# One TensorE step per retention chunk: outputs, update and scores joined, orders planned anew

## The chip, the cores and the metric

The kernel runs on one core of a Trainium2 chip. The metric is device time of one execution in microseconds (us). The engines are TensorE (PE in the profile; its weight loads PEld), VectorE (DVE), ScalarE (ACT), GpSimd (POOL) and the queue of SyncE (SP), which issues nearly all DMA transfers. Each engine works through its own instructions in the order of the program and waits on semaphores for the others.

## The reference

One layer with two head groups side by side. The input is normalised, one projection gives all columns, the groups are gated and mapped back:

```python
h = rms_norm(x, norm_w)
rq, rk, rv, rg, sq, sk, sv, sg = split(h @ w_in)
# A) retention, 4 heads, dk 64, dv 128, 16 chunks of 128 tokens
scores = einsum('bhnid,bhnjd->bhnij', qc, kc) * decay
intra  = einsum('bhnij,bhnje->bhnie', scores, vc)
kv     = einsum('bhnjd,bhnje->nbhde', kc * zeta, vc)
prev   = scan(state = chunk_decay * state + kv_n)     # the state before each chunk
cross  = einsum('bhnid,nbhde->bhnie', qc * xi, prev)
ro = group_norm(intra + cross) * ret_norm_w * silu(rg)
# B) attention in a sliding window of 128, 8 heads over 2 key heads, bias, sinks
so = sliding_window_attention(sq, sk, sv, ...) * silu(sg)
x = x + concat(ro, so) @ w_out
```

There are 2048 tokens and 1024 model columns, all in float32.

## The kernel before

*The big products.* The four projections (three column ranges of w_in, then w_out) are made by Strassen's seven products of half-size blocks, over 8 pairs of token chunks. Each factor is split into a high and a low part (fp32r), and three products of parts make one. They appear in the profile as `acc<-w,x`: 128-row, 128-column products with 512, 384 or 256 columns of result. The splits (`x<-x`, `w<-w`) and the additions around them are work of ScalarE and VectorE.

*Between them* lies the rest, in small products on parts of the array: for each chunk a turn of the keys (`m<-ident,kn`), the attention logits (`m<-ks,qT`, 64x32 parts, in two halves of 32 records in the trace), for each pair of chunks the attention values (`m<-pT,vn`, 32x64 parts), and for each chunk of the retention, on 64x64 parts, in halves of 64 tokens:

- *update*: keys times values (`m<-v,qk`), for each half of the chunk; VectorE adds each to the running state (`state`), two additions of 128x256 for a chunk; for every fourth chunk ScalarE rescales the state (`base`);
- *scores*: keys times queries within each half (`m<-qkT`), and the queries times the state before each half (`m<-state,qkT`); VectorE then multiplies the scores by a triangle (`sT<-m,tri`), two instructions;
- *outputs*: the scores times the values (`m<-v,sT`), accumulated onto the cross products in the same two banks of PSUM; ScalarE moves them out (`ro<-m`, one instruction for one bank and two for the other), VectorE takes their statistics, and once in four chunks follows the group norm.

Queries and keys reach TensorE turned (`qkT`): ScalarE sorts their 16-bit halves apart (`apart`), a transfer stores them (`planes_dram<-apart`), and a transposing transfer brings them back. The values of a chunk are two loads (`v0`, `v1`).

*What sets the order.* The whole program is a list of operations, each with an estimated cost on its engine, its buffers and a due time; `Program.emit` (lines 176 to 329) plays a schedule and writes the instructions of all five engines in the order that it finds, once and for all. It holds back an operation whose buffers are not free; buffers come from shared counts (`SHARE`, `CAP`), PSUM has eight banks, of which small products may hold six (`"rest": 6`) and the big ones three. Operations of TensorE that use parts of the array carry a mark (`"quarters"`, `"eighths"`, `"bands"`); a change between marks, or to none, is charged `CHANGE` or `LESSER`, and `LATER`, `CROWD`, `MOST` and `SOONER` decide how long such an operation may be put off to stand beside another one. `AHEAD` and `SPARE` set how early a load may be issued. `HELD` names results that stay in SBUF instead of going through DRAM, `TURNED` what is turned by DMA. `WIN`, `RET`, `GATE` and `LEAD` (lines 1541 to 1545) are the due times of attention, retention and gates.

In `retention` (from line 907) one loop over the 16 chunks issues, for each, loads, the rotary phase, the key scales and the turn, and then update, state additions, scores, decays, outputs and evacuation, each as an operation of its own. So each chunk has three operations of TensorE, `update` (line 1004), `scores` (line 1051) and `outputs` (line 1075), due at different times and put where the schedule finds room. All instructions pass through one helper, so the profile gives line 421 for nearly every one; the names of the tiles tell them apart.

Of the kernel before, what the change touches and what calls it, by code (L numbers as in the profile page):

```python
# [33 lines left out]
AF = mybir.ActivationFunctionType  # L34
# [28 lines left out]
SHARE = {"x": 8, "raw": 64, "acc": 59, "wr": 32, "wh": 18, "att": 47, "ret": 41, "rin": 56, "gate": 13, "mix": 28, "norm": 5, "res": 3, "turned": 6, "vn": 3, "first": 5, "block": 3, "rest": 6}  # L63
# [3 lines left out]
AHEAD, SPARE, SPARED = 14.0, 3, ("raw", "wr")  # L67
# [36 lines left out]
LATER, CROWD, MOST, SOONER = 0.25, 0.25, 5, 142.0  # L104
# [239 lines left out]
HELD = {"sums": ((3, 1), (5, 4), (5, 5), (6, 3), (6, 6), (7, 0), (7, 1), (7, 5)), "ro": (1, 4, 6, 9, 12, 13, 14, 15), "q": (0, 2, 3, 13, 14), "gates": (4, 7), "so": (2, 5, 15)}  # L344
# [25 lines left out]
def small(n=1):  # L370
    return {"V": (0.2 * n, 0.28 * n, True)}
# [22 lines left out]
VALUES = {"T": (2.05, 2.27, False)}  # L394
# [30 lines left out]
def layer(ctx, tc, xt, xfirst, xtok, nw, w_in, w_rn, qkw, sinks, biasg, rope, decays, dmask, gpow, w_out, out):  # L425
# [33 lines left out]
    def ps(share="rest", name="m"):  # L459
        return Buf("bank", None, F32, name, share)  # L460
# [446 lines left out]
    def retention(at):  # L907
# [15 lines left out]
        state = None  # L923
        st = None
        for c in range(NCH):
# [61 lines left out]
            halves = (slice(0, 64), slice(64, 128))  # L987

            last = c == NCH - 1
            pkv = [ps() for _ in range(1 if last else 2)]  # L990

            def go(e, pkv=pkv, qk=qk, v=v):
# [9 lines left out]
            news = [hb("state") for _ in pkv]  # L1002
# [4 lines left out]
            states = [state]  # L1007
            for p, new in zip(pkv, news):
                old = states[-1]
                op(  # L1010
                    {"V": dve(256)},
                    lambda e, new=new, p=p, old=old: e.tensor_tensor(new(), p()[:, 0:256], old(), ALU.add)
                    if old else e.tensor_copy(new(), p()[:, 0:256]),
                    [p] + [old] * (old is not None), [new], due - 0.5, label="state",
                )
                states.append(new)
            state = states[-1]
            if c % BASED == BASED - 1 and not last:

                def go(e, state=state):  # L1020
                    for pr in range(2):
                        s = state()[:, pr * P : (pr + 1) * P]
                        e.activation(s, s, AF.Copy, scale=gp()[:, pr : pr + 1])

                op({"A": (0.45, 0.55, False)}, go, [state, gp], [state], due - 0.4, label="base")

            pros, sT = [ps(), ps()], hb("sT")
            sTs = [Part(sT, lambda t, i=i: t[:, i * P : (i + 1) * P]) for i in range(2)]

            def go(e, pros=pros, qkT=qkT, states=states):  # L1030
# [22 lines left out]
            for i in range(2):  # L1053
                op(
                    {"V": dve(128)},
                    lambda e, sT=sTs[i], pro=pros[i]: e.tensor_tensor(
                        sT().rearrange("p (a k) -> p a k", a=2), pro()[:, 256:384].rearrange("p (a k) -> p a k", a=2),
                        tri().unsqueeze(1).to_broadcast([P, 2, HALF]), ALU.mult,
                    ),
                    [pros[i], tri], [sTs[i]], due + 0.5, label="decay", also=(sT,),  # L1060
                )

            def go(e, pros=pros, sTs=sTs, v=v, c=c):
# [14 lines left out]
            ro = kb("ro", "mix" if c in HELD["ro"] else "ret")  # L1078
            for i, moves in enumerate([[(slice(0, P), slice(0, P))], [halves, halves[::-1]]]):

                def go(e, ro=ro, pro=pros[i], i=i, moves=moves):
                    for to, of in moves:
                        e.activation(
                            ro()[to, :].rearrange("p (a b d) -> p a b d", a=2, b=2)[:, :, i, :],
                            pro()[of, 0:256].rearrange("p (a d) -> p a d", a=2), AF.Copy,
                        )

                n = len(moves)
                op({"A": (0.307 * n, 0.31 * n + 0.11, False)}, go, [pros[i]], [ro], due + 0.7, label="ro")
            if c % NORMED == 0:  # L1090
                st, ros = sb("st", [P, NORMED, RH, 6]), []
            ros.append((c, ro))

            def go(e, st=st, ro=ro, c=c):
                for h in range(RH):
                    e.bn_stats(st()[:, c % NORMED, h, :], ro()[:, h * P : (h + 1) * P])

            op({"V": (0.8, 0.9, False)}, go, [ro], [st], due + 0.8, label="stats")
            if c % NORMED == NORMED - 1:
                group_norm(st, ros, due + 1)  # L1100
# [81 lines left out]
    def values(c, held, due):  # L1182
# [29 lines left out]
        for k in range(2):  # L1212
# [9 lines left out]
            op({"A": (0.95, 1.05, False)}, go, pavs, [so], due + 2.1, label="so")  # L1222
# [55 lines left out]
    def attend(c, a, b, fac, facs, due, bias_t, ks_t, nsnk):  # L1278
# [112 lines left out]
        for g in range(KVH):  # L1391
            if slot == 0:
                wholes[g] = wide("pT")
            lg, pT = lgs[g], Part(wholes[g], lambda t: t[:, slot * 640 : slot * 640 + 640])
            op(
                {"V": (0.85, 0.95, False)}, lambda e, lg=lg, pT=pT: e.transpose(pT(), lg()), [weights_of[g], weights_of[2 + g]], [pT],
                due + 1.3 + 0.3 * g, label="turn weights", also=(lg, wholes[g]),
            )
            pTs.append(pT)
# [128 lines left out]
    retention(lambda c: RET[0] + c // 2 * 2 * RET[1] + c % 2 * 1.0)  # L1528
# [12 lines left out]
WIN = (58.0, 4.8)  # L1541
RET = (126.5, 2.15)
GATE = (139.0, 5.45)

LEAD = 12.0
# [95 lines left out]
```

## Time and profile before

| | us |
|---|---|
| three timed runs | 675.07, 679.26, 678.53 |
| their median | 678.53 |
| the profiled execution | 676.0 |
| its span in the trace | 674.2 |
| TensorE busy, of the span | 667.9 |
| VectorE busy | 592.8 |
| ScalarE busy | 475.0 |

The profile is of one execution. A row of a view by groups gives the operation, the tiles that it writes and reads, the shape, the count, the busy time and the mean duration of one in ns, and the idle time ahead with what ended it. A row of the timeline gives start, duration, engine and the merged instructions. Each small fp32 product of the program shows as two records of TensorE, so a group of eight products has 16. Durations in the timeline overlap, since the products are pipelined; differences of starts do not.

### The profile page before, as it was taken

Reading aid. Unit: us, or ns where it says so; the run is one execution under the profiler, and the core shown is the slowest. Engines: PE = TensorE matmul, PEld = TensorE weight load, DVE = VectorE, ACT = ScalarE, POOL = GpSimd, SP = SyncE. Lnnn points to the kernel's source line nnn. Section 1 sums busy time; section 2 is a strip of 40 time slices with the busy share of each in tenths; the row PEclk is TensorE's granted clock in tenths of the full one; section 3 lists DMA queues with packets and bytes.
Section 4 is the critical chain, followed back from the end, with each engine's and each line's share of the span. In section 5 each row is a group of like instructions: output and inputs, shape, how many; then the busy total and the mean of one; then the engine's idle time right before and its main releaser. Section 6 shows DMA issues by size and latency. Waiting matters only on the chain.

```text
span 674.2 us, 16326 instructions
## 1 busy us (share of the span) xinstructions
PE 667.9 (99%) x5948; PEld 558.8 (83%) x5948; DVE 592.8 (88%) x1369; ACT 475.0 (70%) x1145; POOL 17.7 (3%) x39
## 2 busy tenths in 40 slices
PE   9999999999999999999999999999999999999998
PEld 7887888888989999998887777777788888888886
DVE  6998967887899988899999989998899999987782
ACT  7663798657797776787989799897999944533300
POOL 0000000033200000000000000000000000000000
PEclk9999999999999999999999999999999999999999
DMA  9976598978975899999989879988996886015652
GB/s 328 367 230 221 180 360 276 344 242 298 251 214 160 253 269 287 310 282 318 270 213 285 234 243 281 197 276 231 313 256 209 224 205 195 17 64 192 215 186 94
DMA packets 154145, 161.65 MB, mean 240 GB/s; under 512 B 67793, under 2 KB 95313, under 8 KB 154065
## 3 DMA queue, kind: packets, MB, share of 16 engines
q1 hardware_dynamic: 153920, 160.60, 79.3%
q8 instruction: 47, 0.77, 0.5%
q14 instruction: 34, 0.27, 0.1%
q10 hardware_dynamic: 144, 0.00, 0.0%
HBM read 97.05 MB, written 49.35 MB: 217 GB/s over the span
## 4 chain that ended last, share of the span: by engine, by line
PE 89%; DMA 4%; DVE 3%; ACT 1%; issue 1%; SPq 0%; DVEq 0%; ACTq 0%
PE acc L421 78%; PE m L421 12%; DMA aq_dram<-r 1%; DMA s_dram<-x 1%; DMA aq_dram<-t 1%; DVE w L421 1%; DVE x L421 1%; DMA xk<-in_xtok 1%; DVE t L421 0%; SPq L421 0%; DMA x<-in_xt 0%; ACT sq L421 0%; DVE s L421 0%; DVE hs L421 0%; ACT x L421 0%
## 5 line engine op out<-in xcount | busy, mean ns | idle before, releaser
L421 PE MATMUL acc<-w,x 128*128 128x512 f32 (+1 forms) x2700 | 594.8, 378 | 0.8 <-ACT x L421 0.4
L421 PEld LDWEIGHTS acc<-w,x 128*128 128x128 f32 x2700 | 490.5, 188 | 89.6 <-issue 7.4
L421 DVE TENSOR_TENSOR x<-x 128x512 fp32r<-128x512 f32 (+2 forms) x220 | 143.5, 674 | 10.6 <-ACT x L421 7.4
L421 ACT ACTIVATE x<-x 128x512 fp32r<-128x512 f32 (+1 forms) x187 | 111.7, 616 | 23.3 <-DVE x L421 15.1
L421 ACT ACTIVATE lg<-lg,nm 128x160 f32<-128x160 f32 x128 | 53.1, 418 | 12.2 <-DVE nm L421 12.2
L421 DVE TENSOR_TENSOR w<-w 128x512 fp32r<-128x512 f32 (+3 forms) x96 | 60.9, 655 | 0.0
L421 DVE SCALAR_TENSOR_TENSOR w<-w,nw_sb 128x512 fp32r<-128x512 f32 (+3 forms) x72 | 49.4, 702 | 1.0 <-ACT w L421 1.0
L421 DVE TENSOR_TENSOR s<-acc,s 128x512 f32<-128x512 f32 (+1 forms) x64 | 41.7, 652 | 8.4 <-PE acc L421 7.7
L421 ACT ACTIVATE w<-w 128x512 fp32r<-128x512 f32 (+1 forms) x72 | 40.7, 599 | 10.3 <-PE acc L421 6.5
L421 DVE CUSTOM_DVE_ANT_0 lg<-m,bias,nsnk 128x160 f32<-128x160 f32 x128 | 40.6, 379 | 5.5 <-PE m L421 5.2
L421 DVE TENSOR_TENSOR r<-acc,t 128x512 f32<-128x512 f32 (+1 forms) x32 | 20.9, 654 | 15.3 <-PE acc L421 13.9
L421 DVE TENSOR_TENSOR t<-acc,t 128x512 f32<-128x512 f32 (+2 forms) x33 | 21.1, 638 | 13.2 <-PE acc L421 12.9
L421 ACT ACTIVATE s<-acc 128x512 f32<-128x512 f32 (+1 forms) x32 | 18.2, 569 | 16.4 <-PE acc L421 14.5
L421 ACT ACTIVATE w<-w,nw_sb 128x512 fp32r<-128x512 f32 (+3 forms) x42 | 27.3, 680 | 2.5 <-DMA w<-in_w_in 1.4
L421 ACT ACTIVATE x<-go 128x512 fp32r<-128x512 f32 x27 | 16.5, 629 | 15.9 <-PE acc L421 9.7
L421 DVE TENSOR_TENSOR t<-acc,s 128x512 f32<-128x512 f32 (+1 forms) x32 | 20.8, 649 | 7.7 <-PE acc L421 6.1
L421 ACT ACTIVATE xk<-xk 128x512 f32<-128x512 f32 x32 | 19.9, 622 | 8.7 <-DMA xk<-in_xtok 8.7
L421 DVE STREAM_TRANSPOSE pT<-lg 128x640 f32<-128x640 f32 x32 | 25.8, 828 | 0.1
L421 ACT ACTIVATE ro<-ro,nmu,rg 128x128 f32<-128x128 f32 x64 | 25.1, 487 | 0.8 <-DVE nmu L421 0.7
L421 ACT ACTIVATION_READ_ACCUMULATOR lg<-lg,nm 128x1 f32 x128 | 24.2, 189 | 0.0
L421 ACT ACTIVATE ro<-m 64x256 f32<-64x256 f32 (+2 forms) x54 | 21.6, 400 | 2.6 <-PE m L421 1.7
L421 ACT ACTIVATE apart<-qn 128x1024 uint16<-128x1024 uint16 x16 | 16.7, 1050 | 8.0 <-DVE qn L421 7.9
(145 smaller groups left out, 589.7 us busy)
## 6 DMA issues: line engine op xcount, KB each, us to landing
x<-in_xt SPq DMA_DIRECT2D x80, 256.0 KB, 4.6
planes_dram<-apart SPq DMA_DIRECT2D x54, 256.0 KB, 3.6
x<-s_dram SPq DMA_DIRECT2D x48, 256.0 KB, 4.0
w<-in_w_in SPq DMA_DIRECT2D x40, 256.0 KB, 5.2
xk<-in_xtok SPq DMA_DIRECT2D x32, 256.0 KB, 4.6
res<-in_xtok SPq DMA_DIRECT2D x32, 256.0 KB, 3.3
s_dram<-x SPq DMA_DIRECT2D x24, 256.0 KB, 3.4
w<-in_w_out SPq DMA_DIRECT2D x20, 256.0 KB, 4.1
```

The lines of the kernel that those rows point to most:

```text
L421: return lambda *a, **k: self.order.put(op(*a, **k))
```

## The change

The loop over chunks now only loads, rotates, scales and turns, and notes the tiles in `chunks`. A second loop runs over steps -1 to 16. A step is one operation of TensorE that issues, without a break, the outputs of chunk c-1, the update of chunk c+1 and the scores of chunk c. Behind it come the evacuation of chunk c-1, the decays of chunk c and the state additions of chunk c+1. The products themselves, their operands and their number stay. The due times of the retention are evenly spaced, where they came in pairs; and the numbers with which the order is planned are others, so that every engine's order differs. Results held in SBUF and chunks turned by TensorE or DMA are partly others (`HELD`, `TURNED`).

```diff
-SHARE = {"x": 8, "raw": 64, "acc": 59, "wr": 32, "wh": 18, "att": 47, "ret": 41, "rin": 56, "gate": 13, "mix": 28, "norm": 5, "res": 3, "turned": 6, "vn": 3, "first": 5, "block": 3, "rest": 6}
+SHARE = {"x": 8, "raw": 57, "acc": 54, "wr": 49, "wh": 18, "att": 54, "ret": 35, "rin": 61, "gate": 6, "mix": 28, "norm": 5, "res": 3, "turned": 12, "vn": 3, "first": 5, "block": 3, "rest": 6}
-AHEAD, SPARE, SPARED = 14.0, 3, ("raw", "wr")
+AHEAD, SPARE, SPARED = 14.5, 4, ("raw", "wr")
-LATER, CROWD, MOST, SOONER = 0.25, 0.25, 5, 142.0
+LATER, CROWD, MOST, SOONER = 0.5, 0.0, 7, 62.0
-HELD = {"sums": ((3, 1), (5, 4), (5, 5), (6, 3), (6, 6), (7, 0), (7, 1), (7, 5)), "ro": (1, 4, 6, 9, 12, 13, 14, 15), "q": (0, 2, 3, 13, 14), "gates": (4, 7), "so": (2, 5, 15)}
+HELD = {"sums": ((3, 1), (5, 4), (5, 5), (6, 3), (6, 6), (7, 0), (7, 1), (7, 5)), "ro": (1, 4, 8, 9, 10, 12, 13, 14, 15), "q": (0, 3, 13, 14), "gates": (1, 7), "so": (2, 14, 15)}
-TURNED = {"q": range(NCH), "qk": range(NCH), "gated": (0, 2, 7, 11, 13, 14)}
-EARLIER_Q, EARLIER_K = 0.0, 10.0
-SCALED = (3.0, 2.6)
+TURNED = {"q": range(NCH), "qk": range(NCH), "gated": (0, 2, 4, 7, 8, 13)}
+EARLIER_Q, EARLIER_K = 0.0, 11.0
+SCALED = (1.0, 2.75)
...
-            op(
-                f32(P, 2), go, [qk, v0, v1], pkv, due - 1.0, "quarters", label="update", also=(v, *news),
-                many=16 * len(pkv),
-            )
...
-            op(
-                f32(P, 2.5 if c == 0 else 3.2), go, [qkT] + [t for t in states[:2] if t], pros,
-                due + 0.4, "quarters", label="scores", also=(sT,), many=48 if c == 0 else 64,
-            )
...
-            op(
-                f32(P, 2), go, [*sTs, v0, v1], pros, due + 0.6, "quarters",
-                label="outputs", also=(v, sT), many=32,
-            )
...
+            chunks.append((c, qk, qkT, v, v0, v1))
...
+        for step in range(-1, NCH + 1):
+            due = at(step)
+            made, reads, writes, also, many = [], [], [], [], 0
+            if step > 0:
+                done = outputs(step - 1, *inside[:2])
...
+            if step < NCH - 1:
+                go, r, pkv, a, n = update(step + 1)
...
+            if 0 <= step < NCH:
+                go, r, pros, sT, n = scores(step, ready[step])
...
+            op(
+                f32(P, many), go, list(dict.fromkeys(reads)), writes, due + 0.4, "quarters", label="step", also=also,
+                many=int(16 * many),
+            )
+            if step > 0:
+                evacuate(step - 1, inside[0], due)
...
-    retention(lambda c: RET[0] + c // 2 * 2 * RET[1] + c % 2 * 1.0)
+    retention(lambda c: RET[0] + c * RET[1])
...
-WIN = (58.0, 4.8)
-RET = (126.5, 2.15)
-GATE = (139.0, 5.45)
+WIN = (58.5, 4.8)
+RET = (124.5, 2.15)
+GATE = (139.0, 5.65)
...
-LEAD = 12.0
+LEAD = 7.0
```

The new helpers `outputs`, `update` and `scores` return the same products as before, with what they read and write; `evacuate` holds the instructions that moved the outputs out and took their statistics before. Four estimated costs change as well, which enter the plan alone: small VectorE operations 0.2 to 0.09, the turn of the softmax weights 0.85 to 0.76, the attention values 2.05 to 2.26, their evacuation 0.95 to 0.65.

More of the change, by code (lines that the diff above doesn't have):

```diff
@@ L922, in retention @@
         )
-        state = None
-        st = None
+        chunks = []
         for c in range(NCH):
@@ L1000, in go, with scores @@
                             )
-            news = [hb("state") for _ in pkv]
-            op(
-                f32(P, 2), go, [qk, v0, v1], pkv, due - 1.0, "quarters", label="update", also=(v, *news),
-                many=16 * len(pkv),
-            )
-            states = [state]
-            for p, new in zip(pkv, news):
-                old = states[-1]
-                op(
[L1011 to L1014, printed above, removed]
-                )
[L1016 to L1025, printed above, removed]
+            return go, [qk, v0, v1], pkv, [v], 2 * len(pkv) / 2
+        def scores(c, states):
+            _, _, qkT, *_ = chunks[c]
             pros, sT = [ps(), ps()], hb("sT")
-            sTs = [Part(sT, lambda t, i=i: t[:, i * P : (i + 1) * P]) for i in range(2)]
-            def go(e, pros=pros, qkT=qkT, states=states):
+            def go(e):
                 for pr in range(2):
@@ L1047, in go, with outputs @@
                                 )
-            op(
-                f32(P, 2.5 if c == 0 else 3.2), go, [qkT] + [t for t in states[:2] if t], pros,
-                due + 0.4, "quarters", label="scores", also=(sT,), many=48 if c == 0 else 64,
-            )
[L1053 to L1063, printed above, removed]
+            return go, [qkT] + [t for t in states[:2] if t], pros, sT, 2.5 if c == 0 else 3.2
+        def outputs(c, pros, sTs):
+            *_, v, v0, v1 = chunks[c]
+            def go(e):
                 for pr in range(2):
@@ L1090, in retention @@
[L1090 to L1100, printed above, removed]
+            return go, [*sTs, v0, v1], pros, [v], 2
@@ L1395, in attend @@
             op(
-                {"V": (0.85, 0.95, False)}, lambda e, lg=lg, pT=pT: e.transpose(pT(), lg()), [weights_of[g], weights_of[2 + g]], [pT],
+                {"V": (0.76, 0.85, False)}, lambda e, lg=lg, pT=pT: e.transpose(pT(), lg()), [weights_of[g], weights_of[2 + g]], [pT],
                 due + 1.3 + 0.3 * g, label="turn weights", also=(lg, wholes[g]),
```

95 lines of the change are left out of this document (78 added, 17 removed).

## The prediction

> **What bounds the kernel now.** I read the page from the top, then the busy time of each engine by stage, then what TensorE waited for, and last its timeline in the retention part.
>
> ```profile
> span 674.2 us, 16326 instructions
> ...
> PE 667.9 (99%) x5948; PEld 558.8 (83%) x5948; DVE 592.8 (88%) x1369; ACT 475.0 (70%) x1145; POOL 17.7 (3%) x39
> ...
> PE 89%; DMA 4%; DVE 3%; ACT 1%; issue 1%; SPq 0%; DVEq 0%; ACTq 0%
> ```
>
> TensorE (PE) is busy for all but 6.3 us of the span, and the chain of work that ended last is TensorE for 89%. A busy TensorE is not one at its peak, though, so the question is what it is busy with. The whole list of what it waited for is short:
>
> ```profile
> PE m L421 <- DVE none L421: 1.2, 1, 1.2
> PE acc L421 <- ACT x L421: 0.4, 1, 0.4
> PE acc L421 <- ACT s L421: 0.4, 1, 0.4
> PE m L421 <- DVE nm L421: 0.4, 1, 0.4
> PE m L421 <- issue: 0.4, 1, 0.4
> PE m L421 <- PE acc L421: 0.3, 1, 0.3
> ```
>
> Beyond the start (1.2) that is 1.9 us in 674. No shorter wait is left to be removed; time can only come out of what TensorE executes, or go in where a new wait appears. By stage, with the retention part in the middle:
>
> ```profile
> 308.00:362.00 54.00, 53.88 (x760) 42.74 (x758) 51.39 (x135) 45.57 (x136) 0.00 (x0) 1.00 0.94 270
> 362.00:487.00 125.00, 124.50 (x1567) 95.53 (x1568) 115.48 (x339) 112.92 (x266) 0.00 (x0) 1.00 0.91 255
> 487.00:529.00 42.00, 42.00 (x201) 34.74 (x199) 40.89 (x89) 41.16 (x74) 0.00 (x0) 1.00 0.81 230
> ```
>
> The columns are the stretch, its length, then busy time of PE, PEld, DVE, ACT and POOL, the granted clock and the DMA share. VectorE (DVE) has 9.5 us idle in the 125 of the retention part, ScalarE (ACT) 12.1, the DMA engines 9%. So the others are close behind TensorE, but behind.
>
> **What a small stretch costs TensorE.** The change moves no matrix product in or out; it groups them. What a break costs is read from start to start in the timeline:
>
> ```profile
> 446.74 0.46 PE L421 MATMUL m<-qkT 64*64 64x64 f32 x16
> 447.02 0.62 PE L421 MATMUL m<-state,qkT 64*64 64x128 f32 x16
> 447.57 0.96 PE L421 MATMUL acc<-w,x 128*128 128x512 f32 x3
> 448.47 0.67 PE L421 MATMUL m<-v,qk 64*64 64x128 f32 x16
> 448.95 0.62 PE L421 MATMUL m<-v,sT 64*64 64x128 f32 x16
> 449.50 2.33 PE L421 MATMUL acc<-w,x 128*128 128x512 f32 x9
> 451.76 0.46 PE L421 MATMUL m<-qkT 64*64 64x64 f32 x16
> 452.05 0.62 PE L421 MATMUL m<-state,qkT 64*64 64x128 f32 x16
> 452.48 1.05 PE L421 MATMUL m<-v,qk 64*64 64x128 f32 x24
> ```
>
> Nine big products (acc) take 451.76 - 449.50 = 2.26 us, three take 448.47 - 447.57 = 0.90. The six between are 1.36, or 0.227 each; three would be 0.68, so 0.22 is the price of going from 128-row products into the 64-row ones. The cross products (state,qkT) take 452.48 - 452.05 = 0.43 when 64-row work follows, and 447.57 - 447.02 = 0.55 when a big product follows: 0.12 for going back. And the first group of a stretch is 0.05 dearer: the update (v,qk) takes 448.95 - 448.47 = 0.48, against 0.43 in the middle. Together 0.39 us per stretch, of which 0.17 lie inside it. After a long run of big products, and after transposes and logits, the entry differs:
>
> ```profile
> 422.79 8.49 PE L421 MATMUL acc<-w,x 128*128 128x512 f32 x36
> 431.22 0.46 PE L421 MATMUL m<-qkT 64*64 64x64 f32 x16
> ...
> 356.76 0.27 PE L421 MATMUL m<-ident,kn 128*128 128x128 f32 x1
> 356.79 1.63 PE L421 MATMUL acc<-w,x 128*128 128x512 f32 x6
> ...
> 377.42 0.27 PE L421 MATMUL m<-ident,kn 128*128 128x128 f32 x1
> 377.62 0.46 PE L421 MATMUL m<-qkT 64*64 64x64 f32 x16
> ...
> 382.13 0.77 PE L421 MATMUL m<-ks,qT 64*32 64x160 f32 x32
> 382.83 0.46 PE L421 MATMUL m<-qkT 64*64 64x64 f32 x16
> ...
> 340.50 1.34 PE L421 MATMUL m<-ks,qT 64*32 64x160 f32 x64
> 341.77 0.67 PE L421 MATMUL m<-v,qk 64*64 64x128 f32 x16
> ...
> 485.13 1.10 PE L421 MATMUL m<-v,sT 64*64 64x128 f32 x32
> ```
>
> 36 big products cost 8.43, or 0.27 over 36 x 0.227 = 8.16. A transpose delays a big product by 0.03, 64-row work by 0.20, so 0.17 there. A half of the logits (32 records) takes 0.70 and a whole 1.27, so a logits stretch has 2 x 0.70 - 1.27 = 0.13 of its own.
>
> **The change, part by part.** *The step.* Between the first 64-row retention stretch (at 341.77) and the last (485.13), the timeline of before has 31 of them: 26 entered from big products, 3 from logits, 2 from transposes. The changed program has one per step, steps -1 to 16, which its order of instructions confirms: 18, of which 17 are entered from big products and 1 from logits. So 13 stretches fewer at 0.17 inside = 2.2; 9 entries from big products fewer at 0.22 to 0.27 = 2.0 to 2.4, I take 2.2; 2 entries from transposes fewer at 0.17 = 0.3. The step saves 4.7 us, 4.5 to 5.0 by the ends.
>
> [...]
>
> *The new order of everything else.* Logits stand in 17 stretches instead of 19: 2 x 0.13 = 0.3 less. Entries of logits and transposes differ by one or two either way, at 0.1 to 0.2 each; I take nothing and keep 0.2 either way. Products, splits and turns are the same in number; one retention output fewer and one query block more go through DRAM, so the 670 transfers of the SP queue stay 670. That order could also lose or shift the 1.9 us of waits above; I count none of it in the sum.
>
> *The update, moved one step forward.* It needs the values (two loads) and the scaled keys of chunk c+1 one step earlier, and both state additions must then be done before the next step's cross products. *The outputs, moved one step back,* hold two banks of PSUM over the gap, and a step writes six of the eight. What follows each step on VectorE and ScalarE:
>
> ```profile
> L421 DVE TENSOR_TENSOR state<-m,state 128x256 f32<-128x256 f32 x30 | 12.5, 415 | 0.7 <-PE m L421 0.4
> L421 ACT ACTIVATE ro<-m 64x256 f32<-64x256 f32 x32 | 12.1, 380 | 0.6
> L421 DVE TENSOR_TENSOR sT<-m,tri 128x128 f32<-128x128 f32 x32 | 8.0, 282 | 0.7 <-PE m L421 0.7
> L421 ACT ACTIVATE ro<-m 128x256 f32<-128x256 f32 x16 | 5.9, 370 | 2.0 <-PE m L421 1.7 <-DMA ro_dram<-ro 0.3
> L421 ACT ACT_TABLE_LOAD x2 | 2.6, 1283 | 1.2 <-PEq L1629 1.2
> ```
>
> Two state additions and two decays are 2 x 0.415 + 2 x 0.282 = 1.39 us of VectorE. The shortest cover between two full steps in the changed order is 12 big products, 12 x 0.227 = 2.7 us, so 1.3 us stay for whatever else is queued there; before, scores and outputs of one chunk had as few as the three big products at 447.57 between them. I price it at nothing; without the cover it is at most 1.39 per step. The evacuation (0.37 + 2 x 0.38 = 1.13 of ScalarE) is the same work at another place. ScalarE gets two more table loads, since gates begin before the last softmax: 2 x 1.28 = 2.6, inside its 12.1 idle, so nothing; uncovered, 2.6.
>
> *The sum.* -4.7 - 0.3 = -5.0, with -5.5 and -4.6 as the ends of TensorE's own part. The profiled execution took 676.0 (span 674.2 and 1.8 around it). The timed runs are 675.07, 679.26 and 678.53, median 678.53; with the profiled one the middle of four is 677.3. From there the forecast is 672.3.
>
> **The rivals.** *Waits join the saving (faster than forecast).* If the new order also sheds the 1.9 us of waits, 677.3 - 5.0 - 1.9 = 670.4; from the lowest run, 668.2. For it: a scores group waited twice at its start (0.3 and 0.4, TensorE's list). Against: those waits are single.
>
> *The gain is given back (no change).* If VectorE rather than TensorE sets the pace of the retention part once that is 5 us shorter, part returns. It has 9.5 idle in the 125 and 1.1 in the 42 after it, so it would have to lose about half of that idle to take 2.5 or more back: 675 to 677.
>
> *Steps wait (slower).* A step has five sets of operands, and the last to arrive sets its start. The one that comes by the longest way is the turned query and key, qkT, written out and turned back by DMA:
>
> ```profile
> L421 SPq DMA_TRANSPOSE qkT<-planes_dram x16: 1226/1288/2542, 331.3 to 452.3; - x16
> ...
> DMA to landing us min/median/max: 3.2/4.2/5.6
> ```
>
> Landings spread by 5.6 - 4.2 = 1.4 us over the median. TensorE takes its stream in order, so behind a late step stand the next big products, and behind them VectorE's additions and the buffers that the loads wait for. Sixteen steps that wait 0.31 us eat the 5.0; from (5.0 + 6.8) / 16 = 0.74 each the kernel is over 1% slower; at 1.4 each it is 677.3 - 5.0 + 22.4 = 694.7. Against it: TensorE waited for no transfer at all before, at a DMA share of 0.91, and its list has nothing of that kind. [...]
>
> That the change doesn't do what it says is excluded by the order of instructions: 14 steps hold all four groups without a break.
>
> **How the numbers follow.** Forecast as summed 0.60, at 672.3, its own range 670 to 675.5; waits join 0.17, at 668 to 670.5; given back 0.09, at 675 to 677; slower 0.14, at 684 to 695. The range reaches down to 668 and up to 679, which leaves out the last and little else. 1%, about what a measurement of this kernel can tell from no change, is 6.8 us of 678.53, and the bound 671.7 cuts the forecast near its middle: 0.28 of it lie below, 0.32 above. Faster by over 1%: 0.28 + 0.17 = 0.45. Within: 0.32 + 0.09 = 0.41. Slower: 0.14.
>
> **What would show it.** In the profile after: 18 retention stretches, groups at 0.43 to 0.48 us and cross products still 0.55 before a big product; TensorE's busy time near 662.9 and its waits still about 3 us; the four groups' counts unchanged. If TensorE's busy time falls by 5 and the span does not, the rows to look at are its waits for sT, state or qkT. I am wrong if the entry cost goes with the number of records rather than of stretches, or if waits of over 0.3 us stand before most steps.

## The result and the profile after

The changed kernel took 673.81 us (median of 4 runs, 673.14 to 674.04) beside 678.15 for the kernel before (4 runs): a ratio of 0.9944, interval 0.9924 to 0.9963. The forecast was 672.3. But the size of this gain did not hold. The unchanged kernel was measured twice more, in later sets, each beside its own runs of the kernel before:

| set | kernel | us, median (lowest to highest, runs) | before, us (runs) | ratio [interval] | span of its profile |
|---|---|---|---|---|---|
| first | changed | 673.81 (673.14 to 674.04, 4) | 678.15 (4) | 0.9944 [0.9924, 0.9963] | 672.2 |
| third | changed, again | 676.67 (674.39 to 679.36, 12) | 677.71 (17) | 0.9979 [0.9964, 0.9994] | 672.7 |
| fourth | changed, a third time | 678.32 (676.46 to 680.02, 12) | 677.75 (22) | 1.0002 [0.9988, 1.0017] | 674.7 |

The first and the last interval do not overlap, and none of the 24 later runs is as fast as the slowest of the first four (674.04). (The second set holds only edited kernels beside the one before. The third set ran on another chip than the second and the fourth; for the first result that is not known.) What can be said is a gain between nothing and 0.6% by these three ratios, where TensorE has, by the prediction's counts, 5.0 us, or 0.7%, less to do. So the question is where the rest went. The page of the first profile after:

```profile
span 672.2 us, 16349 instructions
...
PE 663.9 (99%) x5948; PEld 560.2 (83%) x5948; DVE 589.9 (88%) x1369; ACT 475.6 (71%) x1147; POOL 16.7 (2%) x39
...
PE 87%; DMA 4%; DVE 4%; ACT 3%; issue 1%; SPq 1%; ACTq 0%; DVEq 0%
```

TensorE's busy time fell by 4.0 (from 667.9), the span by 2.0. In the chain that ended last, ScalarE went from 1% to 3% and VectorE from 3% to 4%. What TensorE waited for (us in total, times, longest):

```profile
PE m L421 <- ACT ro L421: 1.0, 2, 0.6
PE acc L421 <- DVE x L421: 0.9, 2, 0.5
PE m L421 <- ACT ks L421: 0.6, 1, 0.6
PE acc L421 <- ACT x L421: 0.5, 1, 0.5
PE m L421 <- issue: 0.5, 2, 0.2
PE acc L421 <- DVE t L421: 0.3, 1, 0.3
```

The start (1.2 again) left out, that is 3.8 us, where it was 1.9. No row of it names a transfer, and no wait is that of a step for one of its operands. By stage:

```profile
362.00:487.00 125.00, 122.20 (x1540) 97.13 (x1533) 114.58 (x336) 113.17 (x259) 0.00 (x0) 1.00 0.88 244
...
408.00:430.00 22.00, 20.25 (x278) 15.48 (x280) 18.95 (x52) 21.39 (x54) 0.00 (x0) 1.00 0.83 248
```

The new idle time lies in the retention part: 2.8 us of the 125, against 0.5 before; in the stages ahead of it and behind it, 308 to 362 and 487 to 529, TensorE has none. The second row is a piece of it in which TensorE idles 1.75 of 22 us while ScalarE is busy for 21.39.

**The step itself does what was forecast.** TensorE's timeline there, with an undisturbed pair of steps below:

```profile
417.49 0.67 PE L421 MATMUL m<-v,sT 64*64 64x128 f32 x16
...
419.61 0.70 PE L421 MATMUL acc<-w,x 128*128 128x512 f32 x2 [0.34 <-DVE t L421]
420.72 2.59 PE L421 MATMUL acc<-w,x 128*128 128x512 f32 x10 [0.41 <-DVE x L421]
423.24 0.67 PE L421 MATMUL m<-v,sT 64*64 64x128 f32 x16
...
425.49 0.73 PE L421 MATMUL acc<-w,x 128*128 128x512 f32 x2 [0.48 <-ACT x L421]
426.74 2.57 PE L421 MATMUL acc<-w,x 128*128 128x512 f32 x10 [0.51 <-DVE x L421]
429.24 0.67 PE L421 MATMUL m<-v,sT 64*64 64x128 f32 x16
...
449.77 0.67 PE L421 MATMUL m<-v,sT 64*64 64x128 f32 x16
450.26 0.62 PE L421 MATMUL m<-v,qk 64*64 64x128 f32 x16
...
450.93 0.62 PE L421 MATMUL m<-state,qkT 64*64 64x128 f32 x16
451.48 3.01 PE L421 MATMUL acc<-w,x 128*128 128x512 f32 x12
454.42 0.67 PE L421 MATMUL m<-v,sT 64*64 64x128 f32 x16
```

In the lower pair, outputs take 450.26 - 449.77 = 0.49 and the cross products 451.48 - 450.93 = 0.55, as said. A whole step with 12 big products behind it takes 454.42 - 449.77 = 4.65. The two steps above have 12 behind each as well and should take 9.30; they take 429.24 - 417.49 = 11.75. So 2.45 us are lost at this one place, and by waits of the *big* products, not of the step: for the addition (t) that empties the bank they write to, and for parts of their factors (x). This is the piece with the shortest cover, on which the prediction had put no price.

**Why the big products are late there.** The rows are from the timelines of ScalarE, VectorE and the SP queue, in that order:

```profile
408.17 6.27 ACT L421 ACTIVATE ro<-ro,nmu,rg 128x128 f32<-128x128 f32 x16
...
423.63 1.15 ACT L421 ACTIVATE ro<-m 128x256 f32<-128x256 f32 x3
424.81 0.63 ACT L421 ACTIVATE x<-x 128x512 fp32r<-128x512 f32 x1
```

```profile
418.77 0.69 DVE L421 TENSOR_TENSOR t<-acc,s 128x512 f32<-128x512 f32 x1 [1.61 <-DMA ro_dram<-ro]
```

```profile
414.98 0.40 SPq L421 DMA_DIRECT2D ro_dram<-ro  x1
```

Two things meet. ScalarE spends 6.27 us on a group norm and then has a queue; the split (x) that TensorE awaits at 425.49 starts at 424.81, right behind an evacuation. And VectorE stood still for 1.61 us, until 418.77, though it had work, because its result t goes into a buffer whose stored content (ro) had not yet left: the second of two stores of it was issued at 414.98, 3.8 us earlier. The split (x) and the next sum (t) follow behind it in VectorE's timeline, from 419.98 and 420.92, so they were late too.

A second place is the attention values behind the step at 388, here in the changed kernel; the first rows are TensorE's, the others ScalarE's:

```profile
391.45 0.43 PE L421 MATMUL m<-pT,vn 32*64 32x128 f32 x4
392.50 0.43 PE L421 MATMUL m<-pT,vn 32*64 32x128 f32 x4 [0.61 <-ACT ro L421]
393.29 2.50 PE L421 MATMUL m<-pT,vn 32*64 32x128 f32 x136 [0.36 <-ACT ro L421]
395.73 1.66 PE L421 MATMUL acc<-w,x 128*128 128x512 f32 x6
```

```profile
390.16 1.28 ACT L421 ACT_TABLE_LOAD   x1
391.45 0.72 ACT L421 ACTIVATE g<-g,rstd_all 128x512 f32<-128x512 f32 x1
392.08 1.16 ACT L421 ACTIVATE ro<-m 128x256 f32<-128x256 f32 x3
```

These 144 records take 395.73 - 391.45 = 4.28 here. Undisturbed they take 2.49 (in the kernel "one_end" below, where they start at 394.67 and the big products behind them at 397.16). So 1.8 are lost, waiting until the evacuation of the step's outputs (ro) has run, and ScalarE does a table load and a gate right before it. With the 2.45 this is 4.2 us, of the 5.0 that were to be saved.

**And why does the gain differ by the set?** Up to the first turn of the keys (m<-ident,kn), TensorE has the same instructions in the same order in both kernels. When it gets there differs from execution to execution, and that leaves the rest of the span as follows:

| profiled execution | first key turn at | span | rest |
|---|---|---|---|
| before | 165.50 | 674.2 | 508.7 |
| before, one more buffer | 163.66 | 673.3 | 509.6 |
| changed | 163.49 | 672.2 | 508.7 |
| changed, again | 163.95 | 672.7 | 508.8 |
| changed, a third time | 165.12 | 674.7 | 509.6 |
| changed, one more buffer | 163.43 | 669.8 | 506.4 |
| the same, again | 164.53 | 672.5 | 508.0 |

Between the profile of before and that of after, the whole difference of 2.0 us lies ahead of the first change in TensorE's order; behind it, both take 508.7. Whether the changed plan of the other engines makes the opening shorter, or chance does, these few executions do not settle: the changed kernel itself has both 163.5 and 165.1. Nor do the profiles show what an ordinary execution of the later sets lost, since the profiled ones (674.48 and 676.46) are about 2 us faster than their medians (676.67 and 678.32). TensorE's busy time behind the first key turn is 504.4 before and 501.6, 501.6 and 502.2 in the three profiles of the changed kernel: it fell by 2.2 to 2.8 there, and the rest of the 4.0 above lies in the opening, where TensorE has the same work.

### The profile page after: what moved, and what is told of

It is laid out like the page before. It is cut to its first block, busy times and chain, and to the rows that moved or that the text cites. A ratio compares the mean times of both kernels' runs of the same rounds, so it can differ in the third digit from the quotient of the medians.

```text
span 672.2 us, 16349 instructions
## 1 busy us (share of the span) xinstructions
PE 663.9 (99%) x5948; PEld 560.2 (83%) x5948; DVE 589.9 (88%) x1369; ACT 475.6 (71%) x1147; POOL 16.7 (2%) x39
## 4 chain that ended last, share of the span: by engine, by line
PE 87%; DMA 4%; DVE 4%; ACT 3%; issue 1%; SPq 1%; ACTq 0%; DVEq 0%
PE acc L421 79%; PE m L421 8%; DMA planes_dram<-apart 2%; SPq L421 1%; DVE w L421 1%; DVE x L421 1%; DMA x<-s_dram 1%; DMA w<-in_w_in 0%; DMA ro_dram<-ro 0%; DMA g_dram<-c 0%; ACT qk L421 0%; ACT so L421 0%; ACT ro L421 0%; ACT apart L421 0%; DVE state L421 0%
## 5 line engine op out<-in xcount | busy, mean ns | idle before, releaser
L421 DVE TENSOR_TENSOR t<-acc,s 128x512 f32<-128x512 f32 (+1 forms) x32 | 20.8, 650 | 8.8 <-PE acc L421 6.7
L421 PE MATMUL m<-pT,vn 32*64 32x128 f32 (+1 forms) x1152 | 21.8, 285 | 1.4 <-ACT ro L421 1.0
```

What stands on the lines that cost most here:

```text
L421: return lambda *a, **k: self.order.put(op(*a, **k))
```

## The experiments

The kernel to which the edits are made is the changed one, unless another is named; "step" is the retention step.

**1. One break per step, or the same product without a break.** Both kernels add one 128-row product to the 13 full steps, into an unused part of a bank. In "one_end" it stands between the step and the big products, where there is a break anyway; in "one_mid" between update and scores, where it makes a second stretch. The planned order of all instructions is otherwise the same in both.

```diff
-            def go(e, made=made):
-                for m in made:
+            full = 0 < step < NCH - 2
+
+            def go(e, made=made, full=full, spare=pkv[0]):
+                for i, m in enumerate(made):
+                    if full and i == 2:    # one_mid; in one_end the product stands behind the loop
+                        e.matmul(spare()[:, 384:512], ident()[:, 0:P], ident()[:, 0:P], start=True, stop=True)
                     m(e)
```

> The changed kernel with one more small product in each of steps 1 to 13: 128 rows by 128 columns, identity times identity, into an unused corner of a bank that the step holds anyway. Here it stands behind the step, next to the big products, so it breaks nothing. Both theories expect the same: 13 times the product itself, 0.1 to 0.3 us each, so 1 to 4 us over the changed kernel. It is the control for the next run.

> The same 13 products, in the same planned order, but inside the step, between the update and the scores, so that the 64-row work stands in 13 stretches more. If a stretch costs TensorE 0.39 us (0.22 in, 0.12 out, 0.05 for the first group), this kernel's TensorE needs 13 x 0.39 = 5.1 us more than with the product behind the step, and the span about as much. If the price goes with the number of records instead, or the time is made up in waits that are there anyway, the two are within 1 us of each other.

Measured: one_end 677.63 (10 runs; ratio 0.9988 [0.9970, 1.0007]), one_mid 678.56 (10 runs; 1.0002 [0.9986, 1.0018]). One step in the timeline of one_mid:

```profile
404.33 0.67 PE L421 MATMUL m<-v,sT 64*64 64x128 f32 x16
...
405.37 0.49 PE L421 MATMUL m<-ident 128*128 128x128 f32 x2
405.79 0.46 PE L421 MATMUL m<-qkT 64*64 64x64 f32 x16
...
412.28 0.67 PE L421 MATMUL m<-v,sT 64*64 64x128 f32 x16
```

and the same in one_end:

```profile
404.20 0.67 PE L421 MATMUL m<-v,sT 64*64 64x128 f32 x16
...
405.90 0.49 PE L421 MATMUL m<-ident 128*128 128x128 f32 x2
406.15 5.73 PE L421 MATMUL acc<-w,x 128*128 128x512 f32 x24
411.80 0.67 PE L421 MATMUL m<-v,sT 64*64 64x128 f32 x16
```

From step to step it is 412.28 - 404.33 = 7.95 against 411.80 - 404.20 = 7.60: 0.35 for a break, a little under the forecast's 0.39. Thirteen are 4.5 us of TensorE. TensorE's busy time differs by 3.5 (671.1 and 667.6), the medians by only 0.9, and even the far ends of the two intervals by no more than 1.0018 - 0.9970 = 0.0048, or 3.3 us. 2.2 us are taken out of the waits that the lists show (3.0 and 0.8). TensorE's list for one_end, without the start:

```profile
PE m L421 <- ACT so L421: 1.4, 1, 1.4
...
PE acc L421 <- DVE x L421: 0.9, 2, 0.5
PE m L421 <- issue: 0.5, 1, 0.5
PE acc L421 <- ACT s L421: 0.2, 1, 0.2
```

These are 3.0 us with the shorter TensorE program; in one_mid, with the longer one, the list beyond the start has a single row, two waits of 0.4 for "issue". (The longest, 1.4 us at 359.11 in one_end, is of a step after all, inside its update and not for one of its operands: what ended it is the evacuation of the attention values, so.) So the price of a break is right, and the branch of the expectation in which the time is made up in waits came true: the step from TensorE's work to the kernel's time fails, and in this part a microsecond given to or taken from TensorE comes through only in part.

**2. Without the table switches.** The gate's SiLU becomes a copy, so that one table load remains of four; the order of instructions is the same. The kernel's result lacks the SiLU.

```diff
-            lambda e: e.activation(g(), g(), AF.Silu, scale=rstd_all()[:, c : c + 1]),
+            lambda e: e.activation(g(), g(), AF.Copy, scale=rstd_all()[:, c : c + 1]),
```

> The changed kernel with the gates' SiLU replaced by a plain copy with the same scale (so the SiLU of both groups is left out of the result): the same instructions in the same order, but ScalarE's table is loaded once instead of four times. Theory: the attention values at 391 to 393 us wait for two banks whose evacuation stands on ScalarE behind a table load of 1.28 us; the 1.7 us that TensorE loses there shrink to 0.4 or less, and the kernel gains 1 to 1.5 us. Rival: the wait comes from the step's six banks alone, since no two are free after a step until all of it is evacuated; then 1.2 us or more stay, and the gain is under 0.5 us.

Measured: 677.26 (12 runs; 0.9976 [0.9955, 0.9996]), within what the changed kernel itself showed (0.9944 to 1.0002). TensorE's attention values behind the step at 390 still lost 0.8 us: 394.04 to 397.37 is 3.33 against 2.49. In the three profiles of the changed kernel the same place lost 1.8, 1.0 and 1.2. So a load is in the way in some executions, but taking the loads out brought no time that can be told from the changed kernel's own spread. (The profiled execution is the slowest of its twelve, 679.13: it has other waits of 1.3 to 1.4 us, and from 424.15 ten big products take 4.06 us, where the changed kernel has 429.24 - 426.74 = 2.50; its page shows the granted clock at 8 tenths in that slice, 423 to 440.) This experiment does not tell whether the wait comes from ScalarE's queue or from the banks that a step holds.

**3. One more buffer.** The stored ro and the sum t share one pool of 83 buffers of 128x512. One more is allocated, while the plan still counts 83, so the order stays the same and only the reuse comes later. The edit was made on the changed kernel (more_1, and more_1b in a later set) and on the kernel before (before_more1).

```diff
-            return sbuf.tile([P, n], b.dtype, tag=b.tag, bufs=CAP[b.tag], name=b.name)
+            return sbuf.tile([P, n], b.dtype, tag=b.tag, bufs=CAP[b.tag] + 1 * (b.tag == "k"), name=b.name)
```

> The changed kernel, with the same order, but one more SBUF buffer of 128x512 behind the 83 that the plan counts with, so that each buffer is taken again one allocation later. Theory: at 418 to 427 us VectorE's addition of a finished product waits 1.6 us for a buffer whose store (the normalised retention outputs) has not landed, and TensorE loses 2.4 us behind it; with the buffer taken one allocation later half of that or more goes, and the kernel gains 1 us or more. Rival: VectorE and ScalarE are simply behind there, and TensorE still loses 2 us or more at that place.

> The changed kernel with one more buffer behind its plan, now beside the changed kernel itself. If the buffer is worth what the first run showed (ratio 0.991 to before), it is 2 us or more under the changed kernel of this set; if that was a matter of the chip and the hour, within 1 us.

> The kernel before, same order, with the one more buffer. Theory: the buffer removes a wait that the changed order brought with it (the kernel before shows no wait of VectorE for a store in the retention part), so it gains under 1.5 us here, and the step's own gain, both with the buffer, is 4 to 6 us. Rival: buffers that are taken again too early cost the kernel before as much as the changed one; then it gains 2 us or more as well, and the step is worth the same 1.5 to 4 us as without it.

Measured: more_1 672.58 (6 runs; 0.9912 [0.9892, 0.9932]); more_1b 674.40 (6 runs; 0.9935 [0.9914, 0.9956]) and, in the same set, before_more1 676.12 (11 runs; 0.9970 [0.9955, 0.9985]) and the changed kernel 678.32. By medians the buffer gives 678.32 - 674.40 = 3.9 us to the changed kernel and 677.75 - 676.12 = 1.6 to the one before; with it, the change is worth 676.12 - 674.40 = 1.7, and the two intervals just touch. The 4 to 6 us that were expected of the step with the buffer did not come. The changed kernel with one more buffer beats the kernel before in both sets, and the changed kernel in the one set that has both; it is the fastest version found. In the retention part (362 to 487) TensorE idles 2.8, 2.0 and 3.6 us in the three profiles of the changed kernel, and 1.1 and 1.7 with the buffer. By place, from start to start (us; the two steps have 12 big products behind each and take 4.65 undisturbed):

| profile | attention values near 390 (undisturbed 2.5) | first of the two steps | second |
|---|---|---|---|
| changed | 4.28 | 5.75 | 6.00 |
| changed, again | 3.45 | 5.50 | 6.04 |
| changed, a third time | 3.65 | 6.38 | 6.01 |
| one more buffer (more_1) | 2.63 | 4.64 | 6.35 |
| the same, again (more_1b) | 3.24 | 4.64 | 8.22 |

The wait of VectorE that had suggested the edit did not go: its t still waits for the stored ro, 1.46 us until 414.90 in more_1 and 1.61 until 416.34 in more_1b. But TensorE's wait for t did. The first of the two steps now loses nothing, where it lost 0.9 to 1.7; the second, which waits for splits (x), loses as much as before or more (in more_1b a clock of 0.50 from 426 to 429 adds an estimated 1.6: its last ten big products take 429.84 - 425.76 = 4.08, and 2.50 in more_1). That is a part of the 3.9 us; where the remainder comes from is not shown.

**4. The two halves of the change.** step_alone has the joined steps with the planning numbers and paired due times of before; plan_alone has the kernel of before, with its three separate operations, and all the new planning numbers, with the retention still due in pairs. In short:

```diff
 step_alone, against the changed kernel
-AHEAD, SPARE, SPARED = 14.5, 4, ("raw", "wr")
-LATER, CROWD, MOST, SOONER = 0.5, 0.0, 7, 62.0
+AHEAD, SPARE, SPARED = 14.0, 3, ("raw", "wr")
+LATER, CROWD, MOST, SOONER = 0.25, 0.25, 5, 142.0
...
-    retention(lambda c: RET[0] + c * RET[1])
+    retention(lambda c: RET[0] + c // 2 * 2 * RET[1] + c % 2 * 1.0)
```

```diff
 plan_alone, against the kernel before
-AHEAD, SPARE, SPARED = 14.0, 3, ("raw", "wr")
-LATER, CROWD, MOST, SOONER = 0.25, 0.25, 5, 142.0
+AHEAD, SPARE, SPARED = 14.5, 4, ("raw", "wr")
+LATER, CROWD, MOST, SOONER = 0.5, 0.0, 7, 62.0
...
```

> The step with the planning numbers of before (shares, leads, due times, held results, estimated costs). By the counts of its order TensorE's work falls by 4.7 us against before: 18 retention stretches of which 16 are entered from big products, and 19 of logits. If the step alone makes the gain, the median is 3 to 5 us under that of before and TensorE's busy time about 663 to 664. If the gain needs the new planning numbers, the waits eat it and the median is within 1.5 us of before.

> Update, scores and outputs apart as before, due in pairs as before, with all the other planning numbers of the changed kernel. Its order has 32 retention stretches, so TensorE's work is that of before within 0.2 us. If the numbers do nothing but fit the step, the median is within 1.5 us of before; if they make part of the gain by removing waits, it is 2 us or more under it; if they suit the step only, it can be 2 us or more above.

Measured: step_alone 693.88 (5 runs; 1.0229 [1.0206, 1.0252]), plan_alone 681.86 (6 runs; 1.0061 [1.0037, 1.0085]). Each half alone is slower than the kernel before. Where step_alone loses its time stands in TensorE's waits and in the windows behind the longest of them:

```profile
PE acc L421 <- ACT x L421: 4.7, 4, 3.8
...
PE m L421 <- DVE ro L421: 3.1, 1, 3.1
PE m L421 <- DVE sT L421: 2.4, 1, 2.4
```

```profile
432.00:438.00 6.00, 6.00 (x75) 4.88 (x76) 6.00 (x18) 5.88 (x15) 0.00 (x0) 0.72 0.93 279
534.00:540.00 6.00, 3.63 (x9) 2.32 (x10) 6.00 (x11) 6.00 (x10) 0.00 (x0) 0.60 0.89 265
540.00:545.00 5.00, 5.00 (x19) 3.97 (x19) 4.44 (x8) 3.89 (x6) 0.00 (x0) 0.80 1.16 196
550.00:556.00 6.00, 1.71 (x7) 0.77 (x5) 6.00 (x11) 3.47 (x5) 0.00 (x0) 0.97 0.58 158
556.00:563.00 7.00, 6.45 (x16) 5.11 (x17) 5.93 (x11) 1.12 (x2) 0.00 (x0) 0.54 0.70 138
```

Three waits of 2.4, 3.1 and 3.8 us (9.3 together) end at 432, 535.6 and 554.8, and behind each the granted clock falls. What that costs is at most the missing share of each stretch (at most, since parts of the second and third pass in shorter waits): 6 x 0.28 = 1.7 behind the first; 6 x 0.40 + 5 x 0.20 = 3.4 behind the second; 6 x 0.03 + 7 x 0.46 = 3.4 behind the third. With the waits that is 17.8 us at most. To be explained are 25.5: the span is 695.0 - 674.2 = 20.8 longer than that of before, and TensorE has, by the counts of the order, 4.7 less to do. The shorter waits of its list come to 5.6, where all those of before were 1.9; some 4 us stay open. The first wait is that of a step for the decays (sT) of the step before it, over three big products; the other two lie behind the retention, where VectorE is busy without a break. The plan is thus not an accompaniment: with a plan that doesn't fit it, the step is the slower case of the prediction, by another way than the one named there.

plan_alone waits 2.15 us until 384.83, when the outputs of a chunk need the decays of its own scores; there too the clock falls, to 0.77, 0.50 and 0.88 in the three stretches of 2 us from 384 on. Its TensorE busy time is 671.6, 3.7 more than before, though its counts had promised the same work; an estimated 1.7 of that is the missing share of the clock, 2 x (0.23 + 0.50 + 0.12), and the remainder is open.

**5. Two other plans.** If ScalarE's queue and the late stores are to blame, a plan that reckons with them should do better. Both were made on the changed kernel with one more buffer: tab4_more1 charges a table switch 4 us instead of 2 when it picks ScalarE's next operation (2 loads instead of 4), st38_more1 reckons with stores that land after 3.8 us instead of 2.6.

```diff
 tab4_more1
-                        s += 2.0
+                        s += 4.0
...
-                    s = s - 2.0 + wait
+                    s = s - 4.0 + wait
```

```diff
 st38_more1
-        op(dma(kbytes), lambda e: e.dma_start(dst(), of(b())), [b], [dst], due, label=f"store {b.name}")
+        occ, _, more = dma(kbytes)["Q"]
+        op({"Q": (occ, 3.8, more)}, lambda e: e.dma_start(dst(), of(b())), [b], [dst], due, label=f"store {b.name}")
```

> The changed kernel with one more SBUF buffer behind the plan, and planned with a dearer switch of ScalarE's table (4 us instead of 2), so that all gates begin after the last softmax and the table is loaded twice instead of four times. TensorE's work stays that of the changed kernel within 0.3 us. If the buffer is what counts, it is at 672 to 673, as the kernel with the buffer alone; if the table loads cost what the waits at 391 us suggested, 1 to 1.5 us less than that.

> The changed kernel with the one more buffer, and planned with stores that land after 3.8 us instead of 2.6 (their measured median is 3.2 to 3.7), so that the plan takes a stored buffer again later. TensorE's work stays the same within 0.1 us. If the plan's error is the landing of stores, the waits near 420 us go and the kernel is 1 to 2 us under the one with the buffer alone. If any new plan brings waits of its own, as the dearer table switch did, it is above it, by up to 10 us.

Measured: tab4_more1 686.31 (5 runs; 1.0122 [1.0102, 1.0142]), st38_more1 692.57 (4 runs; 1.0209 [1.0189, 1.0230]). The first is 12 us above what either branch had; the second went the way of its second branch, but by 18 us and not by up to 10. By the counts of their orders (18 retention stretches in each) TensorE has some 5 us less to do than before in them too. In tab4_more1 the largest loss lies where VectorE is busy without a break:

```profile
560.00:570.00 10.00, 4.98 (x20) 3.42 (x18) 10.00 (x17) 3.90 (x7) 0.00 (x0) 0.86 0.93 275
570.00:580.00 10.00, 8.63 (x25) 6.89 (x26) 7.89 (x14) 1.26 (x2) 0.00 (x0) 0.62 0.53 158
```

TensorE idles for half of the first 10 us, most of it in one wait of 4.3 for a split of w by ScalarE, and then runs at a clock of 0.62. In st38_more1 TensorE waits 7.3 us for x from ScalarE and 5.0 for x from VectorE, spread over ten waits, and its granted clock is 0.96 from 20 to 100 us and 0.99 from 362 to 487, and 1.00 in the other stretches from 100 to 690. Each edit changes the whole order, so neither tells whether table switches or stores cost anything by themselves; what they show is that one planning number moves this kernel by 12 to 18 us (against the 674.40 of more_1b), several times what the step is worth.

**6. The changed kernel again.** No edit; for the spread of its gain, in the table at the top.

> The changed kernel once more, as the control of this set, and to see which of TensorE's waits come back. Theory (single waits differ from execution to execution): the waits of the attention values at 391 to 393 us, 1.0 us in the first profile, are gone or elsewhere, those of the big products near 420 us are there again; the median lies within 1 us of 673.8. Rival (each wait belongs to the order): the same places wait for the same amounts.

> The changed kernel as the control of this set. The two medians so far stand at 0.9944 and 0.9979 of before; a third between 0.993 and 0.999 is expected by every theory, with VectorE's wait for the store of a retention output near 412 and 418 us (0.4 and 1.6 us) and TensorE's waits near 420 and 426 us in its profile again.

Neither median came where it was expected: 676.67 is not within 1 us of 673.8, and the ratio 1.0002 is above 0.999. The places of the losses came back, as the table of experiment 3 shows, but not their amounts: ahead of the first two big products behind the first step TensorE waited 0.34 us for t in the first profile, not at all by the list of the second, and 1.00 in the third. VectorE's wait for the store of ro (1.61 in the first) is in the second profile too, with 1.69; in the third VectorE stands still ahead of the same t for 0.92, but there the profile puts it down to TensorE. So the late store is the cause by two of the three profiles.

## Why the prediction was right in its number, and where its sum was not

- *The price of a stretch* (0.22 in, 0.12 out, 0.05 for the first group): right. The groups of a step take what was read from before, and a break put back costs 0.35. The break goes with the stretch and not with the number of records, since one_mid and one_end have the same ones. The two entries from logits that the step saves stand in the sum at nothing, and the traces agree: a half of the logits takes 382.83 - 382.13 = 0.70 ahead of 64-row work in the kernel before, and 359.02 - 358.32 = 0.70 ahead of a big product in the changed one.
- *Thirteen stretches fewer, -5.0 us of TensorE:* right as far as the counts and the price of a stretch go. The busy time is weak support: it fell by 4.0, near the forecast, but 1.2 of that lie in the opening, whose work is the same. Behind it the fall is 2.2 to 2.8, less than 5.0 partly because some of a wait is shown as busy: two big products between waits are shown with 0.70 to 0.73, where two in a run take 2 x 0.227 = 0.45, and of the 4.2 us lost at the two places only 2.7 are shown as idle.
- *"I count none of it in the sum"*, of the waits that the new order could bring, and *"I price it at nothing"*, of VectorE's work under a cover of 12 big products: this is the step of the sum that failed. The cover held for what was named: in the three profiles of the changed kernel no step waited for its states or decays. But 12 big products of 2.7 us also consume splits, sums and free buffers, and where two such steps follow each other these came late: 2.45 us lost there in the first profile, against a term of nothing. The rows that the prediction named for such a case, the waits for sT, state or qkT, were not the ones; t, x and ro were. The sentence that 1.3 us stay "for whatever else is queued there" had not gone on to list what is queued; the split that was late stood behind an evacuation.
- *Table loads and evacuation at nothing:* not settled. In the first profile one load of 1.28 us stands in the queue ahead of an evacuation on which TensorE waits, but the kernel without these loads was not faster.
- *Given back (0.09):* this rival is what happened, in part, and 0.09 was a small chance for it. It was argued through VectorE's pace over the whole part; what gave back, by the traces, was ScalarE's queue and the reuse of buffers at two places, while VectorE still had 10.4 us idle in the 125. Of these the reuse is backed by an edit (experiment 3), ScalarE's queue by none. Its size, 675 to 677, is the third set's result (676.67).
- *Steps wait for qkT (slower, 0.14):* no profile of the changed order shows such a wait, and none of TensorE's waits in it is put down to a transfer. A slower kernel does come out of the same step with other planning numbers, by way of waits for ScalarE and VectorE and the clock behind them.
- *Waits join the saving (0.17):* no; the waits beyond the start grew from 1.9 to 3.8 us.
- *The start of the sum, 677.3:* it stood well (the later sets have 677.7 to 677.9). But that the opening alone differs by 1.6 to 1.8 us between profiled executions of one order was not known, and it is as large as what is left of the gain. The first result, 673.81, is near the forecast of 672.3 partly by luck: with the help of a short opening, as far as its profiled execution shows. The later medians lie in the stated range of 668 to 679, but 4.4 and 6.0 above the forecast. The likeliest outcome, faster by over 1% (0.45), came in none of the three sets.

Not settled: why the first set's gain is the largest; how much of the wait at the attention values is due to the six banks that a step holds; and where the larger part of the extra buffer's gain comes from.

## What to carry to other kernels

A matrix engine that is busy for 99% of the span is not proof that its work alone sets the time: add a known amount of work to it at no other change (here 4.5 us of breaks) and see how much arrives (here 0.9, and 3.3 at most). When a part of a program is shortened, list for its shortest stretches everything that the *next* consumers need, buffers and neighbours in the queue included, and not only the operands of the step that was moved. And where an order is planned as a whole, weigh an edit of a few tenths of a per cent over several sets of runs, and against what a new plan alone does.

## What the runs showed of the hardware

In the profile of before the granted clock is 1.00 in every stretch up to 671 us, where TensorE's last product ends. The later traces show what a wait costs beyond itself. In step_alone, 2 us behind the end of the wait of 2.4 us, the granted clock is 0.50 (first row); in more_1b it is so, from 426.0 on, behind three short waits in a row at the second of the two steps, of 0.25, 0.55 and 0.51 us (the other rows):

```profile
434.00:436.00 2.00, 2.00 (x20) 1.24 (x13) 2.00 (x8) 2.00 (x7) 0.00 (x0) 0.50 0.86 243
...
425.76 4.15 PE L421 MATMUL acc<-w,x 128*128 128x512 f32 x10 [0.51 <-DVE x L421]
426.00:429.00 3.00, 3.00 (x8) 2.31 (x8) 2.79 (x11) 2.94 (x7) 0.00 (x0) 0.50 1.15 275
```

Behind the second and the third wait of step_alone the clock is 0.50 in all of 536 to 542 and 556 to 562. By these runs the length of a single wait does not decide whether the clock falls. It fell behind waits of 2.38 us (step_alone), 2.15 (plan_alone), 1.44 and 0.41 close together (no_silu) and the three of more_1b. In st38_more1 it fell behind waits of 2.64 (0.96 from 20 to 100 us) and 2.38 (17 big products take 413.80 - 408.36 = 5.44 us, 0.32 each), but not behind 2.43 (46 of them take 471.21 - 460.55 = 10.66, 0.23 each) and 2.20 (1.00 from 556 to 566). What does decide it is not shown here.

In the three profiles of the changed kernel the waits after the start, 0.6 us at most in the first and 1.0 in the third, cost no clock: it is 1.00 in every stretch from 165 to 660 us. But other executions of it did pay: in 6 of the 24 runs of the later sets the mean clock is 0.997, about what a loss of 1.7 us, as in plan_alone, makes of it (1.7 / 677 = 0.0025), while none of the 68 runs of the kernel before beside the second, third and fourth set is under 0.999. By how much this shortened the gain is not settled: those six runs are on average 1.8 us slower than the others of their set in the third, and 0.4 in the fourth.
